# Seven half-width block products in place of eight in the MLP of a decoder block

## The chip, the cores and the metric

One core of one Trainium2 chip runs the whole decoder block in one launch. The metric is the device time of that launch in microseconds (us); less is better. The time before is the median of three runs, and one more execution was profiled.

## What is computed

The block takes x (512 tokens by 1024 channels, float32) and a conditioning vector c. A modulated norm feeds two mixers (a state-space scan and a causal pooling), which gates merge; a projection and a residual follow. Then comes the part that the change touches:

```python
h = rmsnorm(x, norm_mlp_w[i]) * (1.0 + scale_f) + shift_f
x = x + gate_f * (jnp.square(jax.nn.relu(h @ w_up[i])) @ w_down[i])
return rmsnorm(x, norm_final_w)
```

`w_up` is 1024 x 4096 and `w_down` 4096 x 1024, all in float32.

## The kernel before

Channels lie on the 128 partitions and the 512 tokens along the free dimension. TensorE (PE) multiplies float32 data in a format, float32r, that holds fewer bits. So each operand is split into a high part (a cast on ScalarE, ACT) and a low part (the difference, on VectorE, DVE), and each product is made of three: high by high, high by low, low by high (`mm3`, L138 to L142). A column block of 128 outputs over 1024 rows is a `unit` (L144): eight chunks of rows, 24 products of 128 x 128 by 128 x 512, summed in one PSUM bank.

Weights come by `load_unit` (L120): SP issues a load of 512 KB into one of four raw buffers (`RAW`), ACT casts it (L130), DVE subtracts (L131), and the two parts lie in two of the eight buffers of `HL`. A buffer is handed out in the order in which buffers came back, and whoever gets it waits for its last reader. The weights' steps carry a high priority. The order of each engine's queue is laid by the framework's scheduler, from priorities and the order in the program.

PSUM has eight banks. From L617 on all of them are handed out from one list, `PU`.

The MLP (from L706) goes by quarters of the hidden width. In a quarter, eight units of `up` (L713) are made from the modulated activations `h2`; each goes through Relu (ACT, L716), a square (DVE, L708) and a split (L110, L111). Then eight units multiply the quarter's activations `us` with blocks of `w_down`, and `residual` (L659) adds each, times its gate, to `x1` on DVE (L662). The first three `up` units run by halves of the tokens with the rows' chunks outermost (`up_first`, L720), since the second half of the norm is still being worked out; the last three `down` units run by halves too, so that the final norm and the stores of one half lie beside the other half's products (L745 to L760).

The norm ahead (L691 to L701) also goes by halves; `modulate` (L189) makes x * R * scale + shift in two parts, with a temporary tile.

Of the kernel before, what the change touches and what calls it, by code (L numbers as in the profile page):

```python
# [7 lines left out]
F32 = mybir.dt.float32  # L8
# [15 lines left out]
# Columns of the packed per-channel parameters.  # L24
# [11 lines left out]
NSLOT, NRAW, NHL, NPU = 50, 4, 8, 3  # L36
H = T // 2


class Slots:  # L40
    """Buffers of one size, handed out in the order in which they were given back."""
# [17 lines left out]
def block_kernel(tc, xT, crow, arow, par, adaT, wstart, wz, wx, wpool_in, wgate, wpw, wbs, wbp, wout, wup, wdn, out):  # L59
# [3 lines left out]
    with (  # L63
# [6 lines left out]
        def slots(name, n, shape=(P, T), where=sb):  # L70
            def make(i, dt):
                count[0] += 1
                return where.tile(list(shape), dt, tag=f"{name}{i}", name=f"{name}{i}_{count[0]}", bufs=1)
            return Slots(make, n)
# [3 lines left out]
        MT = slots("mt", 3, (P, HG, P))  # L78
        RAW = slots("raw", NRAW, (P, 1024))
        HL = slots("hl", NHL, (P, 1024))  # L80
        SM = slots("sm", 4, (P, NC))
        PU, PS = slots("ps", 8, (P, T), psp), slots("ps", 8, (P, T), psp)
# [8 lines left out]
        cbc = sb.tile([P, DM], F32, name="cbc")  # L91
# [15 lines left out]
        def split(src):  # L107
            """A tile of float32 in two parts that float32r holds exactly."""
            hi, lo = S.get(F32R), S.get(F32R)
            act.copy(hi, src)  # L110
            dve.tensor_tensor(lo, src, hi.bitcast(F32), ALU.subtract)  # L111
            return hi, lo
# [7 lines left out]
        def load_unit(src, n=1024, low=None, at=None, cols=1024):  # L120
            """Blocks of 128 columns of a weight, each in two parts; the buffers are free after their next use."""
            at = at or HL
            with tc.high_priority() if urgent[0] else nullcontext():
                r = RAW.get()
                sp.dma_start(r[:, :n], src)
                blocks, kept = [], []
                for a in range(0, n, cols):
                    w = min(cols, n - a)
                    hi, lo = at.get(F32R), at.get(F32R)
                    act.copy(hi[:, :w], r[:, a:a + w])  # L130
                    (low or dve).tensor_tensor(lo[:, :w], r[:, a:a + w], hi[:, :w].bitcast(F32), ALU.subtract)  # L131
# [56 lines left out]

        def modulate(x, R, scale, shift, hi, lo, t0=0, t1=T):  # L189
            """x * R * scale + shift, in two parts."""  # L190
            t = S.get()
            dve.scalar_tensor_tensor(t[:, t0:t1], x[:, t0:t1], scale, R[:, t0:t1], ALU.mult, ALU.mult)
            act.activation(hi[:, t0:t1], t[:, t0:t1], AF.Identity, bias=shift)
            dve.scalar_tensor_tensor(
                lo[:, t0:t1], t[:, t0:t1], shift, hi[:, t0:t1].bitcast(F32), ALU.add, ALU.subtract)
            S.put(t)

# [8 lines left out]
        def warm(n):  # L206
            """Products of no use that keep the array's clock up."""
# [175 lines left out]
        def bs(g, jp):  # L383
            """Two column blocks of the SSD branch's projection, the rows of one group."""
# [188 lines left out]
        def run(g, fillers):  # L573
            """One group's scan with other units between its steps."""
# [84 lines left out]
        def residual(ps, j, gate, t0=0, t1=T, sums=True, apart=None):  # L659
            """Adds a gated product to x and its squares to the sums."""  # L660
# [12 lines left out]
        def norm(t0, t1, sqs):  # L673
# [3 lines left out]
            bc = rstd(ps, DM, c0, c1, F)  # L677
# [12 lines left out]
        h2 = [(S.get(F32R), S.get(F32R)) for _ in range(8)]  # L690
        for t0, t1 in HALVES:  # L691
# [6 lines left out]
            R = norm(t0, t1, [ssum])  # L698
            for k in range(8):
                modulate(x1[k], R, amod[:, 8 + k:9 + k], mod[:, 24 + k:25 + k], *h2[k], t0, t1)  # L700
# [6 lines left out]
        def squared(u):  # L707
            dve.tensor_tensor(u, u, u, ALU.mult)  # L708
            p = split(u)
            F.put(u)  # L710
            return p

        def up(i):  # L713
            ps = unit(wup[i], h2)
            u = F.get()
            act.activation(u, ps, AF.Relu)  # L716
            PU.put(ps)
            return squared(u)

        def up_first():  # L720
            """The first three units, by halves of the tokens and with the rows' chunks outermost."""
            w = [load_unit(wup[i]) for i in range(3)]
            u = [F.get() for _ in range(3)]
            for t0, t1 in HALVES:
                ps = [PU.get() for _ in range(3)]
                for k in range(8):
                    for i in range(3):
                        mm3(ps[i][:, t0:t1], w[i][k], h2[k], k == 0, k == 7, t0, t1)
                for i in range(3):
                    act.activation(u[i][:, t0:t1], ps[i][:, t0:t1], AF.Relu)  # L730
                PU.put(*ps)
            return [squared(t) for t in u]

        for q in range(4):
            us = up_first() if q == 0 else []
            us += [up(8 * q + i) for i in range(len(us), 8)]
            for j in range(8 if q < 3 else 5):
                ps = unit(wdn[4 * j + q], us)
                residual(ps, j, 40, sums=q == 3)
                PU.put(ps)  # L740
                if q == 3:
                    act.activation(x1[j], x1[j], AF.Copy, scale=col("nfin", j))
            if q < 3:
                free(us)
        w = [load_unit(wdn[4 * j + 3]) for j in (5, 6, 7)]  # L745
        last_sq = F.get()
        for t0, t1 in HALVES:
            for j in (5, 6, 7):
                ps = PU.get()
                for k in range(8):  # L750
                    mm3(ps[:, t0:t1], w[j - 5][k], us[k], k == 0, k == 7, t0, t1)
                residual(ps, j, 40, t0, t1, apart=last_sq if j == 7 else None)
                act.activation(x1[j][:, t0:t1], x1[j][:, t0:t1], AF.Copy, scale=col("nfin", j))
                PU.put(ps)
            R = norm(t0, t1, [ssum, last_sq])
            for j0, j1 in ((0, 2), (2, 4), (4, 6), (6, 8)):
                x = xbig[j0 // 4][:, j0 % 4:j0 % 4 + j1 - j0, t0:t1]
                dve.tensor_tensor(x, x, R[:, t0:t1].unsqueeze(1).broadcast_to([P, j1 - j0, t1 - t0]), ALU.mult)
                sp.dma_start(out[j0:j1, :, t0:t1].rearrange("j p t -> p j t"), x)
            PU.put(R)  # L760
# [71 lines left out]
```

## Time and profile before

| | |
|---|---|
| median of three runs | 1007.04 us (1005.98 to 1007.36) |
| span of the profiled execution (its own time) | 1007.3 us |
| mean granted TensorE clock | 0.996 |
| MLP, from the first full-width `up` unit to the last three units | about 663 to 978 us of the span |
| last three units, final norm and stores | about 978 to 1007 us |
| weights of the MLP | 64 loads of 512 KB, 3.3 us each from issue to landing |

The engines are named PE (TensorE's products), PEld (its weight loads, which overlap the products), DVE, ACT, POOL (GpSimd) and SP (which issues loads). Busy times are shares of the span; rows of slices give tenths of busy time in forty equal pieces. A group of instructions is shown with its line, engine, operation, output and inputs, shapes, count, then its busy time, the mean length of one in ns, and the idle time of the engine ahead of it with what ended that. A timeline row has start, length, engine, line and operation; several equal instructions in a row are merged and counted.

### The profile page before, as it was taken

What the parts mean: (1) busy time and instruction counts of PE and PEld (TensorE: products, weight loads), DVE (VectorE), ACT (ScalarE), POOL (GpSimd) and SP (SyncE); (2) the same over time, 40 slices, a digit from 0 to 9 for tenths busy, and PEclk for the clock granted to TensorE, in tenths of its full rate; (3) what the DMA queues carried; (4) which work ended last, traced back from release to release, by engine and by line L of the source; (5) the groups of instructions that cost most, each with busy time, mean ns of one, the idle gap of its engine ahead of it and who ended that gap; (6) DMA issues with size and microseconds to landing.
All of it is one profiled execution on the core that took longest, in us unless ns stands there. A gap on an engine that the chain in (4) does not pass through costs nothing.

```text
span 1007.3 us, 12196 instructions
## 1 busy us (share of the span) xinstructions
PE 985.8 (98%) x4732; PEld 804.1 (80%) x4732; DVE 623.2 (62%) x887; ACT 482.6 (48%) x718; POOL 85.7 (9%) x79
## 2 busy tenths in 40 slices
PE   9799999999999999999999999999999999999997
PEld 7577777878778878788888888988888888888886
DVE  5978777586777776978765655654344334434444
ACT  5277899579648933453422433442133123213342
POOL 3510310211012012210000000000000000000000
PEclk9999999999999999999999999999999999999998
DMA  9725542452344232437886444032323222232302
GB/s 357 273 89 169 145 126 91 123 130 91 94 129 123 89 111 94 133 102 230 266 266 196 154 161 144 2 126 83 105 86 103 97 92 94 94 105 84 105 1 84
DMA packets 58620, 129.55 MB, mean 129 GB/s; under 512 B 4609, under 2 KB 29313, under 8 KB 58562
## 3 DMA queue, kind: packets, MB, share of 16 engines
q1 hardware_dynamic: 58562, 128.77, 40.0%
q8 instruction: 37, 0.61, 0.2%
q14 instruction: 21, 0.17, 0.1%
HBM read 126.53 MB, written 2.23 MB: 128 GB/s over the span
## 4 chain that ended last, share of the span: by engine, by line
PE 76%; ACT 8%; DVE 7%; DMA 4%; issue 2%; POOL 1%; SPq 1%; DVEq 0%; POOLq 0%; ACTq 0%
PE ps L140 24%; PE ps L141 24%; PE ps L142 24%; DMA mt<-cs_d 3%; ACT hl L130 2%; DVE sz L156 1%; DVE xs L156 1%; ACT L432 1%; PE ps L469 1%; ACT L349 1%; PE ps L453 1%; PE ps L280 1%; DVE hl L131 1%; ACT mt L432 1%; PE ps L446 1%
## 5 line engine op out<-in xcount | busy, mean ns | idle before, releaser
L140 PE MATMUL ps<-s,hl 128*128 128x512 f32 (+1 forms) x1272 | 493.4, 388 | 1.3 <-ACT pad L528 1.2
L141 PE MATMUL ps<-s,hl 128*128 128x512 f32 (+1 forms) x1272 | 488.4, 384 | 0.0
L142 PE MATMUL ps<-s,hl 128*128 128x512 f32 (+1 forms) x1272 | 488.2, 384 | 0.0
L130 ACT CAST hl<-raw 128x1024 fp32r<-128x1024 f32 (+1 forms) x161 | 167.2, 1041 | 285.3 <-PE ps L141 282.6
L140 PEld LDWEIGHTS ps<-s,hl 128*128 128x128 f32 x1272 | 238.9, 188 | 53.3 <-issue 3.5
L142 PEld LDWEIGHTS ps<-s,hl 128*128 128x128 f32 x1272 | 239.0, 188 | 50.2 <-issue 1.0
L141 PEld LDWEIGHTS ps<-s,hl 128*128 128x128 f32 x1272 | 239.1, 188 | 49.4 <-issue 1.4
L131 DVE TENSOR_TENSOR hl<-raw,hl 128x1024 fp32r<-128x1024 f32 x153 | 189.1, 1238 | 130.3 <-ACT hl L130 126.0
L662 DVE SCALAR_TENSOR_TENSOR xs<-ps,mod,xs 128x512 f32<-128x512 f32 (+1 forms) x46 | 31.3, 681 | 110.6 <-PE ps L142 110.5
L110 ACT CAST s<-sz 128x512 fp32r<-128x512 f32 x52 | 31.5, 620 | 52.8 <-DVE sz L708 42.1
L156 DVE CUSTOM_DVE_ANT_0 raw<-raw,cbc,par_t 128x1024 f32<-128x1024 f32 x32 | 40.9, 1279 | 21.2 <-DMA raw<-adaT 21.2
L111 DVE TENSOR_TENSOR s<-sz,s 128x512 fp32r<-128x512 f32 x52 | 35.0, 690 | 22.9 <-ACT s L110 22.9
L432 ACT ACTIVATE mt<-mt,ncs 128x128 f32<-128x128 f32 x128 | 41.7, 392 | 13.6 <-POOL mt L428 13.3
L345 DVE SCALAR_TENSOR_TENSOR s<-ps,par_t,s 128x511 f32<-128x511 f32 (+2 forms) x54 | 40.2, 745 | 7.4 <-ACT s L343 6.8
L280 PE MATMUL ps<-s,hl 128*128 128x512 f32 x144 | 35.1, 397 | 6.4 <-ACT s L265 6.4
L428 POOL TENSOR_SCALAR_AFFINE_SELECT mt<-mt 128x1024 f32<-128x1024 f32 x16 | 19.8, 1244 | 218.0 <-ACT cd L425 117.3
L280 PEld LDWEIGHTS ps<-s,hl 128*128 128x128 f32 x144 | 26.2, 188 | 14.7 <-ACT s L265 9.0
L349 ACT ACT_TABLE_LOAD x19 | 24.4, 1283 | 7.4 <-DVE s L345 7.1
L432 ACT ACT_TABLE_LOAD x20 | 25.7, 1283 | 0.3
L492 POOL TENSOR_TENSOR s<-s 128x256 f32<-128x256 f32 x16 | 17.3, 1082 | 67.9 <-ACT s L491 67.9
L491 ACT ACTIVATE s<-sz 128x512 f32<-128x512 f32 x16 | 10.1, 630 | 26.2 <-DVE sz L490 26.2
L110 ACT CAST s<-s 128x512 fp32r<-128x512 f32 x16 | 9.9, 622 | 25.6 <-DVE s L541 25.3
(164 smaller groups left out, 797.7 us busy)
## 6 DMA issues: line engine op xcount, KB each, us to landing
raw<-adaT SPq DMA_DIRECT2D x32, 512.0 KB, 4.3
raw<-wup SPq DMA_DIRECT2D x32, 512.0 KB, 3.3
raw<-wdn SPq DMA_DIRECT2D x32, 512.0 KB, 3.3
raw<-wx SPq DMA_DIRECT2D x18, 512.0 KB, 3.4
raw<-wz SPq DMA_DIRECT2D x16, 512.0 KB, 4.2
mt<-cs_d SPq DMA_DIRECT2D x16, 512.0 KB, 6.2
raw<-wbs SPq DMA_DIRECT2D x16, 512.0 KB, 3.4
raw<-wgate SPq DMA_DIRECT2D x16, 512.0 KB, 4.0
```

Source lines behind the costliest of these rows:

```text
L110: act.copy(hi, src)
L111: dve.tensor_tensor(lo, src, hi.bitcast(F32), ALU.subtract)
L130: act.copy(hi[:, :w], r[:, a:a + w])
L131: (low or dve).tensor_tensor(lo[:, :w], r[:, a:a + w], hi[:, :w].bitcast(F32), ALU.subtract)
L140: pe.matmul(ps, whi, xhi[:, t0:t1], start=start, stop=False)
L141: pe.matmul(ps, whi, xlo[:, t0:t1], start=False, stop=False)
L142: pe.matmul(ps, wlo, xhi[:, t0:t1], start=False, stop=stop)
L156: dve.tensor_tensor_reduce(r, r, cbc, 1.0, col("b_ada", j), ALU.mult, ALU.add, mod[:, j:j + 1])
L280: pe.matmul(first[u], w[u][i // 2], h[k][i % 2], start=k == 0 and i == 0, stop=k == 7 and i == 2)
L345: dve.scalar_tensor_tensor(t[:, sh:], ps[:, :T - sh], w(3 - sh), t[:, sh:], ALU.mult, ALU.add)
L349: act.activation(o, t, AF.Silu)
L432: act.activation(m[:, i, :], m[:, i, :], AF.Exp, bias=ncs[:, c, g * HG + i:g * HG + i + 1])
```

## The change

Two column blocks are made together. With the rows' chunks taken as even and odd ones and the tokens as two halves, a pair is a product of 2 x 2 blocks by 2 x 2 blocks. In place of eight block products, seven are made, by Winograd's variant of Strassen's scheme, from sums of weight blocks (S1 to S4) and sums of token halves (T1 to T4). A block product is 12 products of 128 x 128 by 128 x 256.

For a pair `prepare` loads a 1 MB weight, laid out by `pairs` on the host, with blocks in the order A21, A11, A12, A22. Two of the weight sums are made by DMAs that add to what lies in the buffer, issued on POOL's queue; two more are sums on DVE. Each of the seven is split in two parts. `sums` makes the token sums on DVE, in place, and splits them; for `h2` that happens once, for the activations in every `up` pair. The square now runs on ACT. The sums of the products are chained in PSUM: a product's result is copied or added, by ACT or DVE, into a bank where the next product goes on adding.

The order of the block products is written in `run_jobs`: `first` of a pair, `close` of the one before, `middle`, `open` of the next, `third`. The first job is `up_first`, now with four blocks by halves. In each quarter the first pair of `down` blocks stays plain (48 products of 512), as do the last four blocks. So 14 pairs of `up` and 10 of `down` change.

The buffers are cut anew: six of the former eight `HL` buffers serve the weights, exactly one pair's six tiles of 1024; A22 has its own two half-size buffers and split tiles. Two PSUM tiles of two banks (`duo`) hold c11 and c12, two banks of one (`AC`) the other two results, and two are left for plain jobs. `hf` keeps the temporaries of `modulate`, from which the float32 activations are made again for the sums.

```diff
+        def sums(u1, u2, t1, t2):
+            dve.tensor_tensor(u1[:, :H], u1[:, :H], u1[:, H:], ALU.subtract)
+            dve.tensor_tensor(u1[:, H:], u2[:, H:], u1[:, H:], ALU.subtract)
+            dve.scalar_tensor_tensor(u2[:, H:], u2[:, H:], -1.0, u1[:, :H], ALU.mult, ALU.subtract)
+            dve.scalar_tensor_tensor(u2[:, :H], u2[:, H:], -1.0, u2[:, :H], ALU.mult, ALU.subtract)
+            two(u1, t1)
+            two(u2, t2)
...
+                y1, y2, y3, y4 = RAW.get(), RAW.get(), RAW.get(), Y4.get()
+                sp.dma_start(y1, w[:, :1024])
+                sp.dma_start(y3[:, T:], w[:, :T])
+                pool.dma_start(y1[:, :T], w[:, 3 * T:], accum_op=ALU.add)
+                pool.dma_start(y3[:, T:], w[:, T:2 * T], accum_op=ALU.add)
+                sp.dma_start(y2[:, T:], w[:, 2 * T:3 * T])
+                sp.dma_start(y4, w[:, 3 * T:])
+                s1, a11 = parts(y1)
+                dve.tensor_tensor(y2[:, :T], y1[:, :T], y1[:, T:], ALU.add)
+                RAW.put(y1)
+                s2, a12 = parts(y2)
+                dve.tensor_tensor(y3[:, :T], y2[:, :T], y2[:, T:], ALU.add)
+                RAW.put(y2)
+                s4, s3 = parts(y3)
+                RAW.put(y3)
+                a22, = parts(y4, T, S)
+                Y4.put(y4)
...
+        def product(ps, a, b, start=False):
+            for m in range(4):
+                w = tuple(x[:, m * P:(m + 1) * P] for x in a)
+                for i, (x, y) in enumerate(((w[0], b[m][0]), (w[0], b[m][1]), (w[1], b[m][0]))):
+                    pe.matmul(ps, x, y, start=start and m == 0 and i == 0, stop=m == 3 and i == 2, skip_group_check=True)
...
+            def open(self):
+                self.be, self.s5 = BE.get(), U5.get()
+                self.c11, self.c12 = self.be[:, 0, :H], self.be[:, 1, :H]
+                product(self.c12, self.a["S1"], self.b["T1"], True)
+                act.copy(self.s5, self.c12)
+            def first(self):
+                self.ac = AC.get()
+                product(self.ac[:, :H], self.a["A11"], self.b["B11"], True)
+                act.copy(self.c11, self.ac[:, :H])
+            def middle(self):
+                product(self.ac[:, :H], self.a["S2"], self.b["T2"])
+                dve.tensor_tensor(self.c12, self.ac[:, :H], self.s5, ALU.add)
+                product(self.c11, self.a["A12"], self.b["B21"])
+            def third(self):
+                product(self.ac[:, :H], self.a["S3"], self.b["T3"])
+                dve.tensor_tensor(self.ac[:, H:], self.ac[:, :H], self.s5, ALU.add)
+                U5.put(self.s5)
+            def close(self):
+                product(self.c12, self.a["S4"], self.b["B22"])
+                self.done(0, self.be[:, :, :H], 1)
+                BE.put(self.be)
+                product(self.ac[:, :H], self.a["A22"], self.b["T4"])
+                self.done(1, self.ac.rearrange("p (a b) -> p a b", a=2), -1)
+                AC.put(self.ac)
...
+        def run_jobs(jobs):
+            last = None
+            jobs[0].prepare()
+            for n, job in enumerate(jobs):
+                after = jobs[n + 1] if n + 1 < len(jobs) else None
+                if after:
+                    after.prepare()
+                if isinstance(job, Pair):
+                    if n == 0 or not isinstance(jobs[n - 1], Pair):
+                        job.open()
+                    job.first()
+                    if last:
+                        last.close()
+                    job.middle()
+                    if isinstance(after, Pair):
+                        after.open()
+                    job.third()
+                    last = job
+                else:
+                    if last:
+                        last.close()
+                    last = None
+                    job.run()
...
+        def activated(q, p, i, ps, sign):
+            u = U.get()
+            act.activation(ab(u), ps, AF.Relu, scale=float(sign))
+            act.activation(u, u, AF.Square)
+            two(u, us[2 * p + i])
+            kept[i] = u
+            if i == 1:
+                sums(kept[0], u, *ust[p])
+                U.put(kept[0], u)
...
+            for k in range(8):
+                act.activation(hf[k], hf[k], AF.Identity, bias=mod[:, 24 + k:25 + k])
+            for m in range(4):
+                sums(*hf[2 * m:2 * m + 2], *h2t[m])
...
+            for b in duo:
+                pe.matmul(b[:, 0, :], h2[0][0][:, :P], h2[0][0], start=True, stop=True)
+            for i in range(4):
+                activated(0, i // 2, i % 2, ab(ps[i]), 1)
...
+        jobs = [Plain(lambda: [load_plain(wup[i // 2], i % 2, *(() if i < 3 else (S, T))) for i in range(4)], up_first)] + [up(0, 2), up(0, 3)]
+        for q in range(3):
+            jobs += [down_plain(q, (0, 1))] + [down(q, p) for p in (1, 2, 3)] + [up(q + 1, p) for p in range(4)]
+        jobs += [down_plain(3, (0, 1)), down(3, 1), down_plain(3, (4,)), Plain(lambda: loads(3, (5, 6, 7)), last_down)]
+        run_jobs(jobs)
```

`two` is an ACT copy into the high part and a DVE difference for the low one. `parts` is `two` on a whole tile of 1024. `done` is `activated` for `up` pairs; for `down` pairs it is one DVE instruction per block that adds the gated result to `x1`, with the negated gate where the sign is -1.

More of the change, by code (lines that the diff above doesn't have):

```diff
@@ L704, in block_kernel @@
             ada(j)
[L707 to L723, printed above, removed]
+        nmod = sb.tile([P, 8], F32, name="nmod")
@@ new lines, in prepare, with parts @@
+        def prepare(w):
+            def parts(y, n=1024, at=HL):
+                hi, lo = at.get(F32R), at.get(F32R)
+                two(y, (hi, lo))
+                at.put(hi, lo)
+                return [(hi[:, o:o + T], lo[:, o:o + T]) for o in range(0, n, T)]
+            with tc.high_priority():
+                y1, y2, y3, y4 = RAW.get(), RAW.get(), RAW.get(), Y4.get()
[15 more added lines that the diff above has]
+                Y4.put(y4)
+            return {"S1": s1, "A11": a11, "S2": s2, "A12": a12, "S4": s4, "S3": s3, "A22": a22}
@@ new lines, in up_first, with up, down, done @@
+            ub.update(moving(us, ust))
+            for b in duo:
+                pe.matmul(b[:, 0, :], h2[0][0][:, :P], h2[0][0], start=True, stop=True)
+            for i in range(4):
+                activated(0, i // 2, i % 2, ab(ps[i]), 1)
+            PU.put(*ps[:2])
+            AC.put(*ps[2:])
+        def up(q, p):
+            return Pair(wup[4 * q + p], hb, lambda i, ps, sign: activated(q, p, i, ps, sign))
+        def down(q, p):
+            def done(i, ps, sign):
+                j = 2 * p + i
+                x = ab(x1[j])
+                g = (mod[:, 40 + j:41 + j], nmod[:, j:j + 1])[sign < 0]
+                dve.scalar_tensor_tensor(x, ps, g, x, ALU.mult, ALU.add)
+                if q == 3:
+                    squares(j)
+            return Pair(wdn[4 * p + q], ub, done)
```

196 lines of the change are left out of this document (145 added, 51 removed).

## The prediction

> **What bounds the kernel now.** I read the page first: its span, its engines, its forty slices and the chain that ended last.
>
> ```profile
> span 1007.3 us, 12196 instructions
> PE 985.8 (98%) x4732; PEld 804.1 (80%) x4732; DVE 623.2 (62%) x887; ACT 482.6 (48%) x718; POOL 85.7 (9%) x79
> ...
> PE   9799999999999999999999999999999999999997
> ...
> DVE  5978777586777776978765655654344334434444
> ACT  5277899579648933453422433442133123213342
> POOL 3510310211012012210000000000000000000000
> ...
> PE 76%; ACT 8%; DVE 7%; DMA 4%; issue 2%; POOL 1%; SPq 1%; DVEq 0%; POOLq 0%; ACTq 0%
> ```
>
> TensorE (PE) has no slice with room in the last third, where the MLP lies; VectorE (DVE) is at 0.3 to 0.4 there, ScalarE (ACT) lower, GpSimd (POOL) empty. So the MLP costs what its products cost. The busy time by stretches gives that price, the timeline that of half-width products:
>
> ```profile
> 663.00:978.00 315.00, 315.00 (x1366) 256.26 (x1365) 132.38 (x150) 98.42 (x125) 0.00 (x0) 1.00 0.28 92
> ```
>
> ```profile
> 978.94 0.28 PE L140 MATMUL ps<-s,hl 128*128 128x256 f32 x1
> 978.94 0.19 PEld L141 LDWEIGHTS ps<-s,hl 128*128 128x128 f32 x1
> 979.05 0.28 PE L141 MATMUL ps<-s,hl 128*128 128x256 f32 x1
> 979.05 0.19 PEld L142 LDWEIGHTS ps<-s,hl 128*128 128x128 f32 x1
> ...
> 987.27 0.29 PE L142 MATMUL ps<-s,hl 128*128 128x256 f32 x1
> ```
>
> ```profile
> 649.79 0.28 PE L140 MATMUL ps<-s,hl 128*128 128x256 f32 x1
> ...
> 656.46 0.28 PE L142 MATMUL ps<-s,hl 128*128 128x256 f32 x1
> ```
>
> The columns of the first are stretch, length, then busy time and count of PE, weight loads, DVE, ACT, POOL, clock, DMA share and GB/s. A 512-wide product takes 315.0 / 1366 = 0.2306 us. The last stage's first half has 72 products 256 wide (three blocks, eight chunks, three products): 8.33 us over 71 steps, 0.117 us. Beside the second norm's work, 57 consecutive ones give 6.67 / 56 = 0.119. I take 0.119: halving the width halves the price, though every product still has its own weight load.
>
> **The products.** A pair of column blocks was 48 products of 512: 11.07 us. It becomes seven block products of 12 products of 256: 84 x 0.119 = 10.0 us (9.8 at 0.117). By the job list 24 of the 32 pairs change: 14 in `up`, 10 in `down`. At PE's pace that is 24 x 1.07 = 25.7 us saved (30 at 0.117). `up_first` runs four blocks by halves, 192 x 0.119 = 22.8 us, where 144 halves and 24 whole ones stood, 17.1 + 5.5 = 22.6: +0.2. The two products that prepare the PSUM banks: +0.5.
>
> **What the other engines must do in those 10 us.** Durations come from the groups of the MLP stretch, the steps of back-to-back ones from the merged timeline.
>
> ```profile
> L131 DVE TENSOR_TENSOR hl<-raw,hl 128x1024 fp32r<-128x1024 f32 x60 | 73.4, 1226 | 78.0 <-ACT hl L130 74.6
> L130 ACT CAST hl<-raw 128x1024 fp32r<-128x1024 f32 x60 | 62.8, 1050 | 177.7 <-PE ps L141 175.5 <-PE ps L142 2.2
> L111 DVE TENSOR_TENSOR s<-sz,s 128x512 fp32r<-128x512 f32 x32 | 22.1, 693 | 19.9 <-ACT s L110 19.9
> L708 DVE TENSOR_TENSOR sz<-sz 128x512 f32<-128x512 f32 x32 | 21.8, 685 | 0.0
> L662 DVE SCALAR_TENSOR_TENSOR xs<-ps,mod,xs 128x512 f32<-128x512 f32 x28 | 21.0, 751 | 87.7 <-PE ps L142 87.7
> L110 ACT CAST s<-sz 128x512 fp32r<-128x512 f32 x32 | 19.9, 621 | 42.1 <-DVE sz L708 42.1
> L716 ACT ACTIVATE sz<-ps 128x512 f32<-128x512 f32 x29 | 17.1, 591 | 0.0
> ...
> L669 ACT ACTIVATE sz<-xs 128x512 f32<-128x512 f32 x3 | 1.9, 634 | 0.0
> ...
> L192 DVE SCALAR_TENSOR_TENSOR s<-xs,amod,ps 128x256 f32<-128x256 f32 x3 | 1.3, 475 | 0.0
> L730 ACT ACTIVATE sz<-ps 128x256 f32<-128x256 f32 x3 | 0.9, 379 | 0.0
> ```
>
> ```profile
> 647.60 1.27 DVE L194 SCALAR_TENSOR_TENSOR s<-s,mod,s 128x256 fp32r<-128x256 f32 x3
> ...
> 658.10 3.50 DVE L131 TENSOR_TENSOR hl<-raw,hl 128x1024 fp32r<-128x1024 f32 x3 [4.80 <-ACT hl L130]
> 661.52 1.89 DVE L708 TENSOR_TENSOR sz<-sz 128x512 f32<-128x512 f32 x3
> ```
>
> Three in a row of 1226 ns end after 3.50 us, so the step is (3.50 - 1.23) / 2 = 1.14; likewise 0.60 for 512 elements and 0.39 for 256. A full DVE queue is priced by steps, one that waits before every instruction by durations.
>
> DVE, an `up` pair: three differences of 1024 and one of 512 for the weights (4.02), two weight sums of 512 (1.20), two 256-wide PSUM adds (0.78), two differences of the activation (1.20), four 256-wide sums (1.56), two more differences (1.20): 9.96 us by steps, 11.4 by durations. A `down` pair has two residuals of 0.75 in place of the last three terms: 7.5 us. ACT, an `up` pair, by durations: casts 3 x 1.05 + 0.62, PSUM copies 2 x 0.38, Relu 2 x 0.59, Square 2 x 0.63, four casts of 0.62: 9.45. So the room that the slices show is used up: DVE equals PE in `up` and is at three quarters in `down`; ACT keeps a little.
>
> When DVE falls behind, its inputs are there and the steps apply, so I choose near the steps: an `up` pair at 10.4 us (bounds 9.9 and 11.4), a `down` pair at 10.05. 24 x 11.07 = 265.7 becomes 14 x 10.4 + 10 x 10.05 = 246.1: -19.6 us.
>
> **New waits on PE.** Inside a row of pairs each read of a bank lies under other products: after `first` come the 24 of `close`; after S2 the 24 of A12 and the next `open`; after S3 the next `first` and S4: each 2.86 us for an add of 0.48 or a copy of 0.38, with perhaps one 1.14 us difference ahead on the queue. Where a pair follows a plain job, nothing lies between `first` and S2: PE waits for the copy, 0.38 and some 0.2 of hand-over, 0.6 x 5 places = 3.0. Where a plain job follows a pair, S3's add has S4 alone over it, 1.43 us: beside a busy DVE I put 0.2 x 5 = 1.0 (0 to 3).
>
> With six weight buffers, exactly one pair, y1 of the next pair is cast only once A11 is done; `close` and `middle` (5.7 us) cover 1.05 + 1.23. After `up_first`, whose chunks are outermost, its first block frees its buffers nine products (1.1 us) before the end, so the first pair waits about 1.3. The token sums for h2t follow the second norm's work on DVE:
>
> ```profile
> 646.42 1.26 DVE L192 SCALAR_TENSOR_TENSOR s<-xs,amod,ps 128x256 f32<-128x256 f32 x3 [0.90 <-PE ps L184]
> ...
> 652.41 0.89 DVE L194 SCALAR_TENSOR_TENSOR s<-s,mod,s 128x256 fp32r<-128x256 f32 x2 [0.19 <-ACT s L193]
> ```
>
> From 653 on 16 sums and 8 differences take 16 x 0.39 + 8 x 0.60 = 11.0 us, to 664; `up_first` covers that, as its 22.8 us from 646 on end at 669. But its four blocks are activated all at once under the first pair: 7.9 us of sums and differences, 5.2 of weights and 0.8 of adds, 13.9 us of DVE against 10.0 of PE. The next pair, with a plain job's weights to prepare, recovers the 3.9. I count 1.5 (0 to 4).
>
> Behind a waiting add on DVE's queue stand the next weights, behind the copy on ACT's the casts of y3 and the Relus: a late add delays the weights that PE wants 5.7 us later, and those have room. The last stage keeps its halves and its norm; its third block takes the buffers of block 4, and two half blocks, 5.7 us, cover that split: nothing.
>
> **The loads.** Per pair 1.75 MB in place of 1.0, some 180 GB/s where the stretch above had 92. Two of the transfers add into a buffer and go through POOL, whose queue is otherwise empty here; no row shows such a transfer. The nearest:
>
> ```profile
> raw<-wup SPq DMA_DIRECT2D x32, 512.0 KB, 3.3
> ...
> sz<-adaT SPq DMA_DIRECT2D x8, 512.0 KB, 9.5
> ...
> s<-xT SPq DMA_DIRECT2D x8, 256.0 KB, 4.3
> ...
> out<-xs SPq DMA_DIRECT2D x8, 256.0 KB, 2.3
> ```
>
> The bounds are 2.3 and 9.5 us; I take 4.3, a 256 KB load beside others. With four raw buffers y1 of a pair takes y3's of two pairs earlier. That loop (load 3.3, add, split 2.3, S1 to the following S4 5.7, split 2.3) is 13.6 us plus the add, and has 20.0: it stalls nothing up to 6.4 us, so zero here. On SP's queue y3's load waits for the y2 buffer of the pair before; load and add (7.6 us) then end about 5 us ahead of their use. On POOL's queue each add waits for its load, and nothing stands behind but the next add.
> No row has the price of a software-issued transfer; the Trainium skill ("DMA: Bandwidth & Descriptors", Anatomy of one DMA) gives about 2.0 us plus the bytes at 436 GB/s. That is an estimate of 2.6 us, and the sum stays as it is.
>
> **The sum.** Against the profiled execution's span, 1007.3, the only time it has (the median is 1007.04): -19.6 + 0.2 + 0.5 + 3.0 + 1.0 + 1.3 + 1.5 = -12.1, so 995.2, and on the median's scale 994.9. Forecast 995, its own range 985 to 1002.
>
> **Rivals.**
> *Nothing waits* (0.13): DVE keeps its steps in all pairs, products run at 0.117 and the edges hide. 24 x (11.07 - 9.83) = 29.8 saved, a few us of edges: 981. For it: PE's rate in the quiet stretch. Against: DVE's 9.96 against 9.83.
> *DVE becomes the bound in `up`* (0.13): each step waits for its cast, 11.4 us a pair: 14 us more than forecast, 1009, no change to speak of. For it: 74.6 us of L131's idle time was waiting for ACT. Against: that DVE had nothing else to do.
> *The adding transfer is late* (0.10), the case on the slow side: over 6.4 us each us costs half a us per pair. From 7.4 us on (12 us over 24 pairs are 0.5 each) the gain is gone; at 9.5 us it is 1.55 x 24 = 37 us on 995: 1032. For it: two transfers in series and a buffer loop over two pairs. Against: the DMA share in the MLP row is 0.28.
> *The order is not the written one* (0.03): the scheduler lays the queues; if the covering products aren't in between, three hand-overs of about 0.6 per pair are bare: 43 us, 1038.
> *Weight loads don't hide* (under 0.01): the rows above start a load of 0.19 us every 0.11 us beside matmuls at the same step. If each load stood alone, a pair would cost 84 x (0.119 + 0.188) = 25.8 against 48 x (0.231 + 0.188) = 20.1 us: 137 us slower than now, 1144.
> The Trainium skill ("TensorE: Matmul & The Clock Gate", Part 3) says that a weight load overlaps running matmuls only where the row groups differ; these loads have all 128 rows. By it the last rival would hold; the trace disagrees, with 0.117 us a product.
>
> **Chances.** The forecast has 0.60. Faster by over 0.2% (about what a measurement of this kernel can tell from no change) means under 1005: forecast, the first rival and a third of the second, 0.77. Within 0.2%: 0.05, out of the second. Slower: 0.18, the rest of the second and the last three. The range, 981 to 1011, leaves out the last three (0.14) and the fast edge of the first (0.06).
>
> **What would show it.** Right: in the stretch of `up` pairs DVE busy nine tenths and more, PE with gaps of under 1 us before products that follow a PSUM add, and about 10.4 us a pair; in `down` about 10.05 and DVE near three quarters; a gap of about 0.6 us on PE at each change from plain job to pair; about 4 us from the adding transfer's issue to its landing. Wrong: PE waiting for weight differences all through `down` (transfer late); a matmul step over 0.125 us; or `up` pairs at 11 us and more.

## The result, and the profile after

| | before | after |
|---|---|---|
| median of four runs each | 1006.92 us (1005.98 to 1007.36) | 1104.74 us (1101.89 to 1107.79) |
| span of the profiled execution | 1007.3 us | 1106.1 us |
| mean granted TensorE clock | 0.996 | 0.961 |

The ratio is 1.098 (95% interval 1.096 to 1.100): the change costs a tenth. The forecast was 995, the range 981 to 1011, and none of the rivals gave this time. The page of the changed kernel, with the lines that answer to those of before:

```profile
span 1106.1 us, 14849 instructions
...
PE 1002.7 (91%) x5622; PEld 856.7 (77%) x5622; DVE 741.3 (67%) x1121; ACT 577.6 (52%) x892; POOL 125.5 (11%) x127
...
PE   8899999999999999998999987898879888887896
...
DVE  6985976667677688877456559565575567555763
ACT  5277987697498234541133337543464346434652
POOL 3600221110120122000000000001101110011000
PEclk9999999999999999999999989899999998988998
```

PE, at nine tenths and more in every slice of the last third but the very last before, stands mostly at seven to nine tenths there now. DVE is at five to seven tenths up to the last slice: no engine is full there. A stage in which nothing is full is bound by waits, so the next thing to look for is who waits for whom.

First, in which stage the time lies. The second norm ends and the final norm begins with products on a tile of ones; these rows of the timeline (start, length, engine, line, operation) give both edges, first before, then after:

```profile
645.68 0.70 PE L184 MATMUL ps<-sz,ones 128*128 128x256 f32 x2
...
987.40 0.28 PE L166 MATMUL ps<-zeros,ones 128*128 128x2 f32 x2
```

```profile
664.21 0.64 PE L195 MATMUL ps<-sz,ones 128*128 128x256 f32 x2
...
1082.12 0.28 PE L177 MATMUL ps<-zeros,ones 128*128 128x2 f32 x2
```

The second of each pair of norm products starts at 646.0 and 664.5. So 18.5 us are lost ahead of the MLP, which the prediction had not priced at all; the MLP goes from 341.4 to 417.6 us, 76.2 more; the rest goes from 19.9 to 24.0. Together that is 98.8. The MLP by stretches (stretch, length, then busy time and count of PE, weight loads, DVE, ACT, POOL, clock, DMA share, GB/s), before and after:

```profile
646.00:987.40 341.40, 341.40 (x1562) 281.46 (x1561) 147.12 (x177) 110.71 (x149) 0.00 (x0) 1.00 0.26 87
```

```profile
664.50:1082.10 417.60, 349.30 (x2447) 327.56 (x2446) 265.39 (x406) 204.49 (x321) 39.05 (x46) 0.93 0.45 115
```

PE idled for none of the 341.4 us before and for 68.3 of the 417.6 after, and the clock fell from 1.00 to 0.93. The waits of that stage (engine and line, what it waited for, us in total, times, longest):

```profile
ACT d L733 <- DMA d<-wup: 57.5, 12, 7.9
...
DVE d L773 <- DMA d<-wdn: 34.1, 10, 5.6
...
PE ps L792 <- ACT duo L810: 22.6, 9, 4.7
PE ps L792 <- DVE ps L819: 21.8, 10, 5.6
```

ACT stands before a cast of weights and DVE before a weight sum because a transfer isn't there, and PE stands before a PSUM copy (L810) and a PSUM add (L819) of these same engines. One lap in a row of pairs shows how the two hang together; the rows are those of the timeline, in order of time:

```profile
885.33 1.22 DVE L734 TENSOR_TENSOR d<-d,d 128x1024 fp32r<-128x1024 f32 x1
...
886.58 0.33 SPq L766 DMA_DIRECT2D d<-wup  x1
...
891.48 0.85 POOL L768 DMA_DIRECT2D d<-wup  x1 [7.10 <-DMA d<-wup]
...
893.88 1.58 PE L792 MATMUL ps<-s,s 128*128 128x256 f32 x12
...
896.44 1.04 ACT L733 CAST d<-d 128x1024 fp32r<-128x1024 f32 x1 [5.58 <-DMA d<-wup]
...
897.39 0.37 ACT L810 COPY duo<-ps 128x256 f32<-128x256 f32 x1
...
897.69 1.03 ACT L733 CAST d<-d 128x1024 fp32r<-128x1024 f32 x1
897.70 2.35 DVE L734 TENSOR_TENSOR d<-d,d 128x1024 fp32r<-128x1024 f32 x2
...
897.81 2.93 PE L792 MATMUL ps<-s,d 128*128 128x256 f32 x12 [2.35 <-ACT duo L810]
...
898.95 0.33 SPq L770 DMA_DIRECT2D d<-wup  x1
...
900.08 0.33 SPq L766 DMA_DIRECT2D d<-wup  x1
...
910.33 1.04 ACT L733 CAST d<-d 128x1024 fp32r<-128x1024 f32 x1 [4.09 <-DMA d<-wup]
```

The split of a y3 ends on DVE at 886.55, and 0.03 us later SP issues the load of a y1 (L766), that of the pair after the next, which takes y3's buffer. 4.9 us on, at 891.48, it is there and POOL issues the adding transfer (L768). That lands 4.9 us later; ACT, idle for 5.58 us ahead of it, casts this y1 at 896.44. Behind that cast, on ACT's queue, have stood c11's copy (897.39), for which PE waits, and the cast of the y3 that comes one pair after the first (897.69). Its split ends at 900.05, and at 900.08 the following y1's load starts. The lap, 13.5 us, is 4.9 + 4.9 + 3.7: a ring of a buffer and an in-order queue, once per pair, where PE's work is 10. SP's queue would close it nearly as soon: a load of a y2 (L770), which takes the buffer of the y1 just split, stands there ahead of the next y1's load, and it is issued at 898.95, 12.4 us after 886.58.

The gap costs more than itself. The stretch in front of the wait, the one behind it, and the next:

```profile
889.00:897.80 8.80, 6.46 (x55) 6.25 (x53) 2.97 (x5) 2.41 (x4) 1.42 (x2) 1.00 0.47 120
897.80:901.20 3.40, 3.39 (x16) 3.39 (x17) 3.28 (x4) 3.40 (x7) 0.29 (x1) 0.50 0.59 110
901.20:905.00 3.80, 3.80 (x34) 3.80 (x34) 3.55 (x7) 3.05 (x6) 0.00 (x0) 1.00 0.70 246
```

For 3.4 us after a gap of 2.35 us the granted clock is 0.50, and 16 products are done in place of some 29. PE's busy time of the last experiment below, whose clock reads 1.00, is 324.0 us in this stage; here it is 349.3. With that kernel as the measure of the products alone, the sum of the MLP is: 341.4 - 17.4 (fewer products) + 25.3 (slow clock) + 68.3 (idle) = 417.6.

The transfers themselves, in the MLP (count, KB each, median us to landing):

```profile
d<-wup POOLq DMA_DIRECT2D x26, 256.0 KB, 4.3
d<-wup SPq DMA_DIRECT2D x12, 512.0 KB, 4.4
d<-wdn POOLq DMA_DIRECT2D x20, 256.0 KB, 5.1
```

### The profile page after: what moved, and what is told of

Same layout as the page of the kernel before. It is cut to its first block, busy times and chain, and to the rows that moved or that the text cites. A ratio compares the mean times of both kernels' runs of the same rounds, so it can differ in the third digit from the quotient of the medians.

```text
span 1106.1 us, 14849 instructions
## 1 busy us (share of the span) xinstructions
PE 1002.7 (91%) x5622; PEld 856.7 (77%) x5622; DVE 741.3 (67%) x1121; ACT 577.6 (52%) x892; POOL 125.5 (11%) x127
## 5 line engine op out<-in xcount | busy, mean ns | idle before, releaser
L151 PE MATMUL ps<-s,d 128*128 128x512 f32 (+1 forms) x670 | 261.0, 390 | 2.9 <-ACT pad L530 1.7
L152 PE MATMUL ps<-s,d 128*128 128x512 f32 (+1 forms) x670 | 256.8, 384 | 0.0
L153 PE MATMUL ps<-s,d 128*128 128x512 f32 (+1 forms) x670 | 256.0, 383 | 0.0
L733 ACT CAST d<-d 128x1024 fp32r<-128x1024 f32 x87 | 90.4, 1047 | 154.9 <-DMA d<-wup 61.7
L141 ACT CAST d<-d 128x1024 fp32r<-128x1024 f32 (+1 forms) x97 | 100.1, 1034 | 106.0 <-PE ps L152 55.0
L151 PEld LDWEIGHTS ps<-s,d 128*128 128x128 f32 x670 | 125.8, 188 | 31.2 <-issue 3.3
L142 DVE TENSOR_TENSOR d<-d,d 128x1024 fp32r<-128x1024 f32 x89 | 111.4, 1254 | 57.2 <-ACT d L141 56.7
L152 PEld LDWEIGHTS ps<-s,d 128*128 128x128 f32 x670 | 126.0, 188 | 25.5 <-issue 2.2
L153 PEld LDWEIGHTS ps<-s,d 128*128 128x128 f32 x670 | 125.9, 188 | 25.6 <-issue 0.9
L734 DVE TENSOR_TENSOR d<-d,d 128x1024 fp32r<-128x1024 f32 x87 | 105.2, 1221 | 49.8 <-ACT d L733 49.5
L792 PE MATMUL ps<-s,d 128*128 128x256 f32 x654 | 98.2, 301 | 27.6 <-ACT duo L810 22.6
L792 PEld LDWEIGHTS ps<-s,d 128*128 128x128 f32 x654 | 90.1, 207 | 30.4 <-ACT duo L810 24.4
L792 PE MATMUL duo<-s,d 128*128 128x256 f32 x684 | 99.0, 291 | 13.6 <-ACT d L733 4.0
L792 PEld LDWEIGHTS duo<-s,d 128*128 128x128 f32 x684 | 90.4, 197 | 18.3 <-ACT d L733 4.9
L773 DVE TENSOR_TENSOR d<-d 128x512 f32<-128x512 f32 x24 | 16.6, 692 | 79.9 <-DMA d<-wdn 34.1
L151 PE MATMUL duo<-s,d 128*128 128x512 f32 (+1 forms) x135 | 53.8, 402 | 4.1 <-DVE xs L627 4.0
L152 PE MATMUL duo<-s,d 128*128 128x512 f32 (+1 forms) x135 | 53.3, 395 | 0.0
L153 PE MATMUL duo<-s,d 128*128 128x512 f32 (+1 forms) x135 | 52.8, 392 | 0.0
L434 ACT ACTIVATE d<-d,ncs 128x128 f32<-128x128 f32 x128 | 41.9, 392 | 10.6 <-POOL d L430 10.4
```

Of the source, the lines that this page charges most:

```text
L151: pe.matmul(ps, whi, xhi[:, t0:t1], start=start, stop=False)
L152: pe.matmul(ps, whi, xlo[:, t0:t1], start=False, stop=False)
L153: pe.matmul(ps, wlo, xhi[:, t0:t1], start=False, stop=stop)
L434: act.activation(m[:, i, :], m[:, i, :], AF.Exp, bias=ncs[:, c, g * HG + i:g * HG + i + 1])
L733: act.copy(dst[0], src)
L734: dve.tensor_tensor(dst[1], src, dst[0].bitcast(F32), ALU.subtract)
```

## The experiments

Theory T is the ring above. Its rivals: R1, the adding transfers as such are too many or too slow; R2, DVE or ACT are simply full. T4 and R4 concern the 18.5 us ahead of the MLP. In the expectations, "85 us of gaps and 27 us of slow clock" are a rougher count than the 68.3 and 25.3 above, from the starts of neighbouring products between 640 and 1085 us of the changed kernel: a long step's excess over the product's own price is a gap, a short one's is slow clock. Each experiment is one run with its profile; the kernel before took 1005.96 to 1008.08 us beside them. The four runs of the changed kernel span 5.9 us, so a difference of that size between two single runs says little. The changed kernel's profile is of its slowest run, 1107.79 us; its row has the median and that profile. The results together, MLP meaning from the second norm's last product on ones to the final norm's first:

| kernel | us | second norm ends | MLP | PE busy in it | clock in it |
|---|---|---|---|---|---|
| before | 1005.96 to 1008.08 | 646.0 | 341.4 | 341.4 | 1.00 |
| changed | 1104.74 | 664.5 | 417.6 | 349.3 | 0.93 |
| no add into y1 | 1039.71 | 659.9 | 355.5 | 332.1 | 0.97 |
| no add into y3 | 1084.65 | 666.0 | 394.5 | 340.0 | 0.95 |
| y1's cast behind y3's | 1097.07 | 664.2 | 408.6 | 346.3 | 0.93 |
| both queues | 1070.81 | 663.4 | 382.0 | 338.6 | 0.96 |
| sums on GpSimd | 1094.02 | 662.1 | 406.6 | 345.3 | 0.94 |
| slots reordered | 1047.27 | 661.1 | 360.9 | 330.1 | 0.98 |
| banks apart | 1085.24 | 650.8 | 412.6 | 348.0 | 0.91 |
| queues and banks | 1044.94 | 655.1 | 367.8 | 331.3 | 0.97 |
| the same, sums on GpSimd | 1041.21 | 648.9 | 371.2 | 336.1 | 0.95 |
| slots, banks, first pair | 1026.72 | 652.1 | 352.5 | 326.3 | 0.99 |
| the same, sums on GpSimd | 1025.08 | 648.7 | 355.3 | 330.8 | 0.97 |
| and y2's sum behind the add | 1022.34 | 653.3 | 347.5 | 326.7 | 0.98 |
| the same, sums on GpSimd | 1017.32 | 649.7 | 346.0 | 324.0 | 1.00 |

**One add away.**

```diff
-                pool.dma_start(y1[:, :T], w[:, 3 * T:], accum_op=ALU.add)
```

> Left out: the adding transfer into y1 (the last column group's half of S1's weight sum). Theory T (a ring): y1's load, its adding transfer, y1's cast, y3's cast queued behind it on ScalarE, y3's split and the next y1's load, which takes y3's slot, close in one lap of about 13.9 us per pair. Without the add the lap is 13.9 - 4.9 = 9.0 us, under PE's 10.3, so 24 pairs fall from about 14.1 to 10.3: 91 us less, about 1015 us (1005 to 1030), and ScalarE's and GpSimd's waits for DMA go. Rival R1 (the two adding transfers as such: traffic and GpSimd's queue): half of the two goes, so about half of the 90 us: 1060, and the same for the other add. Rival R2 (VectorE or ScalarE are simply full): no change, about 1105.

```diff
-                pool.dma_start(y3[:, T:], w[:, T:2 * T], accum_op=ALU.add)
```

> Left out: the adding transfer into y3 (the second column group's half of the weight sum behind S3 and S4). Theory T: it lies beside the ring of y1, not in it, so little moves: 1085 to 1105 us, and ScalarE still waits for y1's add. Rival R1 (the adding transfers as such): as without the add into y1, about 1060. Rival R2 (VectorE or ScalarE full): no change, about 1105.

Without y1's add 65 us go, without y3's 20. The two transfers are alike in size and queue, so R1, which wanted 45 and 45, falls; R2 falls too. T had the order right and the size wrong: the first time is 10 us above its range (1005 to 1030), the second just under its own (1085 to 1105). It had put all of the stage's loss on the ring, and 355.5 us are still 14 above the MLP before.

**The queue's order alone.** The next pair's y1 is held behind this pair's y3, on ACT:

```diff
+                with tc.issue_after(y3_cast.pop()) if y3_cast else nullcontext():
-                s1, a11 = parts(y1)
+                    s1, a11 = parts(y1)
...
                 s4, s3 = parts(y3)
+                y3_cast.append(casts[-1])
```

> Everything is computed; only the order on ScalarE's queue changes: the next pair's y1 cast stands behind this pair's y3 cast (and so behind c11's copy). Theory T: the ring then closes over two pairs, as the prediction had reckoned, and y3's slot comes free without waiting for the next y1: PE's pace, 24 x (14.1 - 10.3) = 91 us less, about 1015 us (1005 to 1040), the same transfers notwithstanding. Rival R1 (the transfers as such are too many or too slow): no change, 1095 to 1110. Rival R2 (VectorE or ScalarE full): no change.

A miss: 8 us, little more than the spread of the changed kernel's runs. The waits of this kernel's MLP say why:

```profile
PE ps L798 <- DVE ps L825: 43.1, 19, 5.6
DVE d L778 <- DMA d<-wup: 32.7, 12, 3.8
DVE d L778 <- DMA d<-wdn: 29.0, 10, 5.7
```

ACT no longer heads the list; the same wait has moved to DVE, where the next pair's y2 sum (L778, it needs y1 with its add) stands ahead of y3's split and of the PSUM add L825. The theory was mended: the ring closes through either queue. So both are opened, by the same means:

```diff
+                cast, rest = y3_cast.pop() if y3_cast else (None, None)
+                with tc.issue_after(cast) if cast else nullcontext(), tc.issue_after(rest) if cast else nullcontext():
-                s1, a11 = parts(y1)
-                dve.tensor_tensor(y2[:, :T], y1[:, :T], y1[:, T:], ALU.add)
+                    s1, a11 = parts(y1)
+                    dve.tensor_tensor(y2[:, :T], y1[:, :T], y1[:, T:], ALU.add)
```

> Everything is computed; the next pair's y1 cast stands behind this pair's y3 cast on ScalarE, and the next pair's y2 sum behind this pair's y3 split on VectorE. Theory T, mended after the order on ScalarE alone gave 8 us: the ring closes through either in-order queue (a y2 sum that waits for y1's add stands ahead of y3's split on VectorE too), so both have to be opened. Then the loop runs over two pairs, and PE's 85 us of gaps and 27 us of slow clock in the MLP shrink to about 30 and 12 as they did without the add into y1: 1025 us (1010 to 1050). Rival R1 (the adding transfers as such are too slow or too many): no change from the order on ScalarE alone, 1090 to 1105.

34 us go, with the same transfers and the same instructions: against R1. It is also less than T gave, 21 us above its range. The lap is 12 us in place of 13.5 (y1's loads at 856.78, 868.73 and 880.62), and in it PE waits for a difference (0.35 us before 869.89) and a residual (1.1 before 872.45) on DVE. That holding y1 behind y3 is what keeps the lap at 12 was not tried by itself.

**No adding transfer.**

```diff
-                sp.dma_start(y3[:, T:], w[:, :T])
-                pool.dma_start(y1[:, :T], w[:, 3 * T:], accum_op=ALU.add)
-                pool.dma_start(y3[:, T:], w[:, T:2 * T], accum_op=ALU.add)
-                sp.dma_start(y2[:, T:], w[:, 2 * T:3 * T])
                 sp.dma_start(y4, w[:, 3 * T:])
+                sp.dma_start(y2[:, T:], w[:, 2 * T:3 * T])
+                pool.tensor_tensor(y3[:, T:], y1[:, :T], y1[:, T:], ALU.add)
+                pool.tensor_tensor(y1[:, :T], y1[:, :T], y4, ALU.add)
```

> Everything is computed; the two weight sums are made by GpSimd's tensor additions of 512 from buffers that are loaded anyway, with no adding transfer and 1.0 MB per pair in place of 1.75; the queues' order is left to the scheduler as in the changed kernel. Theory T: the lap loses the add's 4.9 us and gains two additions of about 1.4 us each: 13.9 - 4.9 + 2.8 = 11.8 us against PE's 10.3: about 1045 us (1030 to 1065). Rival R1 (the transfers as such): as without both, under 1035. If GpSimd's additions hold VectorE up at a shared port, VectorE's own additions grow longer and it is over 1065.

A miss for both, and the clearest word against R1: with no adding transfer and 73 GB/s in the MLP in place of 115, 11 us go. The third branch, a shared port, had the right side (over 1065), but DVE's busy time in the MLP grows by 9.6 us only, its 1024-wide differences keep their mean (1221 ns, 1220 before), and the same sums cost nothing in the kernels further down. The waits of this kernel, 690 to 1060 us:

```profile
POOL d L769 <- DVE d L734: 211.3, 18, 20.5
...
ACT d L733 <- POOL d L770: 40.3, 18, 3.8
```

L769 makes y3's sum and needs the buffer that the pair before's y2 gives back late; L770, y1's sum, stands behind it on POOL's queue, and ACT waits for L770. By these rows the ring has a third queue to close through.

**The slots alone.** The same instructions, the same transfers, no order forced; only the buffers are given back in another sequence, so that the next y1 no longer takes y3's:

```diff
-                RAW.put(y1)
                 s2, a12 = parts(y2)
                 dve.tensor_tensor(y3[:, :T], y2[:, :T], y2[:, T:], ALU.add)
-                RAW.put(y2)
                 s4, s3 = parts(y3)
-                RAW.put(y3)
+                RAW.put(y3, y1, y2)
```

> Everything is computed, with the same instructions; only the order in which a pair gives its three raw buffers back changes, to y3, y1, y2, so that the next pair's y2 takes y3's slot, its y3 takes y1's and the y1 after that takes y2's. Theory T (the ring y3's slot, y1's load, y1's add, y1's cast, y3's cast behind it): y1's load no longer waits for a y3 split, the ring is cut, and the MLP's 85 us of gaps and 27 us of slow clock fall to 40 and 15 or less: about 1045 us (1020 to 1070). Rival R1 (the adding transfers as such): no change, 1090 to 1110. Rival R2 (VectorE or ScalarE full): no change.

1047.27 where 1045 was expected: 57 us of the MLP's 76. This settles that the loop through the buffers cost the time: neither the number of transfers nor any engine's work changed, and the adding ones landed no sooner on the whole (medians 5.3 and 4.5 us here, 4.3 and 5.1 before). On ACT the wait shrinks from 57.5 us to this (690 to 1020 us):

```profile
ACT d L733 <- DMA d<-wup: 21.4, 10, 3.5
```

**The banks.** The changed kernel puts banks 4 to 7 into two tiles of two banks for its whole length. A place ahead of the MLP, where PE stops in a unit:

```profile
518.94 0.39 PE L151 MATMUL duo<-s,d 128*128 128x512 f32 x1
...
522.59 0.68 DVE L627 TENSOR_TENSOR xs<-xs,duo 128x512 f32<-128x512 f32 x1
...
523.32 0.80 PE L151 MATMUL duo<-s,d 128*128 128x512 f32 x1 [3.99 <-DVE xs L627]
```

```diff
-        duo = [psp.tile([P, 2, T], F32, name=f"duo{i}") for i in range(2)]
...
+        duo = [[bank(4 + 2 * i + j, F32) for j in range(2)] for i in range(2)]
...
-                self.c11, self.c12 = self.be[:, 0, :H], self.be[:, 1, :H]
+                self.c11, self.c12 = self.be[0][:, :H], self.be[1][:, :H]
...
-                self.done(0, self.be[:, :, :H], 1)
+                self.done(0, (self.c11, self.c12), 1)
```

> Everything is computed; PSUM banks 4 to 7 are four tiles in place of two two-bank ones over the whole kernel (a pair's first block is then evacuated in two instructions of 256). Theory T4: the 18 us lost ahead of the MLP come from units in the two banks of one tile waiting for each other's evacuation: the lag at the second norm falls from 18 to under 5 us, about 1088 us in all. Rival R4 (the MLP's loads and splits, put at high priority, get in the way earlier): no change ahead of the MLP, about 1105.

As T4 had it. The rows of this kernel:

```profile
650.51 0.64 PE L191 MATMUL ps<-sz,ones 128*128 128x256 f32 x2
...
1063.36 0.28 PE L173 MATMUL ps<-zeros,ones 128*128 128x2 f32 x2
```

13.7 of the 18.5 us ahead of the MLP go and 3.9 of the 4.1 behind it (1083.5 - 1063.4 = 20.1). That the two banks of one tile cost this is shown; that a unit waits for the evacuation of the unit in its tile's other bank is read from the row at 523.32 and not tried by itself. What the last 4.8 us ahead of the MLP are stays open.

**Together.** Both queues and the banks, then the same with sums on GpSimd (the edits above, combined):

> Everything is computed; both queues' order as in the kernel with both queues mended, and banks 4 to 7 as four tiles. Theories T and T4 together: the two gains add up, 1025 - 19 = about 1005 us (990 to 1030). If the transfers as such bound the MLP: about 1075.

> Everything is computed; both queues' order, banks 4 to 7 as four tiles, and the two weight sums on GpSimd in place of the adding transfers. Theory T: with the ring open the sums' way matters little, within 15 us of the same kernel with adding transfers: about 1000 us (985 to 1020). Rival R1 (the adding transfers as such): over 40 us faster than that kernel.

The two gains do add (34 and 20 make 54, 60 were measured), but the queues' own run had stayed 46 us above its expectation, and these stay 40 above theirs with it, outside both ranges. The way of the sums matters little, 4 us, as T has it.

Next the slots in place of the queues, and in `up_first` the two banks evacuated first that the first pair needs. In the changed kernel the first pair waits like this:

```profile
683.10 1.21 PE L792 MATMUL duo<-s,d 128*128 128x256 f32 x8 [1.00 <-DVE d L734]
687.56 0.80 PE L792 MATMUL duo<-s,d 128*128 128x256 f32 x2 [3.25 <-DVE s L734]
692.31 2.93 PE L792 MATMUL ps<-s,d 128*128 128x256 f32 x12 [3.95 <-ACT pad L887]
696.16 0.80 PE L792 MATMUL duo<-s,d 128*128 128x256 f32 x2 [0.92 <-ACT d L733]
```

```diff
-            ps = [PU.get(), PU.get(), AC.get(), AC.get()]
+            ps = [AC.get(), AC.get(), PU.get(), PU.get()]
```

> Everything is computed: the raw buffers given back in the order y3, y1, y2, banks 4 to 7 as four tiles, and up_first evacuating the two banks first that the first pair needs. T and T4 add up: 1045 - 20, and about 8 us for the first pair's wait of over 5 us with the slow clock behind it: 1015 us (990 to 1040). If only the transfers' time counts: 1075.

> Everything is computed: as the kernel with slots, banks and first pair mended, with the two weight sums on GpSimd in place of the adding transfers. T: the ring is cut either way, so within 15 us of it, on the lower side since y1 is whole 6 us after its slot comes free in place of 10: 1005 us (985 to 1030). Rival R1: over 40 us faster than that kernel.

Both lie within their ranges, 12 and 20 us above what was expected, and 2 us apart from each other, which is against R1 once more. Last, y2's sum and what follows from it behind the PSUM add:

```diff
-                dve.tensor_tensor(self.c12, self.ac[:, :H], self.s5, ALU.add)
+                self.add = dve.tensor_tensor(self.c12, self.ac[:, :H], self.s5, ALU.add).ins
...
                     job.middle()
+                    if isinstance(after, Pair):
+                        after.split(job.add)
```

> Everything is computed: the kernel with slots, banks and first pair mended, and on VectorE the next pair's y2 sum and what follows from it stand behind this pair's PSUM add into C12. Theory T (queued waits): PE's waits for PSUM adds, 5 us, and for weight differences, 9 us, shrink with the slow clock behind them: 1012 us (1002 to 1020). Rival R2 (VectorE full in `up`): no change, 1022 to 1030.

> Everything is computed: the same order on VectorE in the kernel with the weight sums on GpSimd. Theory T: the five waits of about 2 us for a PSUM add go, with the slow clock behind them, 9 + 8 us: 1008 us (998 to 1018). Rival R2 (VectorE full in `up`): no change, 1020 to 1030.

4 us with adding transfers, which lies in R2's "no change" (1022 to 1030); 8 us without them, at the upper edge of T's range and under R2's. So this pair doesn't settle whether the last waits are queued ones or DVE being full in `up`; that stays open. The last kernel is the best, 1017.3, and still 1.1% slower than the one before (1006.21 beside it). It loses 3.7 us ahead of the MLP and 4.6 in it. Its PE needs 324.0 us for the MLP and idles for 22; the kernel before needs 341.4 and idles for none. A cost of its own is that GpSimd's additions lengthen DVE's differences (whether PE's last waits come from that wasn't tried). DVE's groups from 690 to 990 us, in this kernel and in the one with adding transfers:

```profile
L730 DVE TENSOR_TENSOR d<-d,d 128x1024 fp32r<-128x1024 f32 x77 | 104.8, 1367 | 12.5 <-ACT d L729 11.9
```

```profile
L730 DVE TENSOR_TENSOR d<-d,d 128x1024 fp32r<-128x1024 f32 x76 | 92.3, 1222 | 27.1 <-ACT d L729 26.9
```

## Why the prediction was wrong

**The step that failed** is in its part on loads: "That loop (...) is 13.6 us plus the add, and has 20.0: it stalls nothing up to 6.4 us, so zero here." It let y3's split wait for buffers and products alone and so gave the loop two pairs. On ACT's queue the cast of y3 stands behind the next pair's y1 cast, which waits for its own load and add, and that load had waited for the y3 before. The loop therefore closes within one pair: 4.9 + 4.9 + 3.7 = 13.5 us of 10, where the text had 20. Cutting it by the buffers' order alone gave back 57 of the MLP's 76 us. The prediction did say, just before, what stands behind a waiting add and a waiting copy; it did not ask what stands behind a cast that waits for a transfer. The rival of the late adding transfer named the ring's parts, but hung on a duration over 6.4 us; the adds landed in 4.3 and 5.1 (medians), close to the 4.3 chosen, and of 48 only two took over 6.4 (6.8). The rival on the scheduler's order looked at PE's queue; it was the order on ACT's, DVE's and POOL's that counted.

**Not in the sum at all.** Losing the clock: a term for a wait was its length, and behind most gaps of over 2 us came 3.4 us and more at half clock, which cost 25 us in the MLP. The stages ahead of the MLP: the diff showed that banks 4 to 7 became two tiles for the whole kernel, and the text priced only the two products that prepare them, at 0.5 us; the tiles cost 13.7 ahead and 3.9 behind.

**Mis-sized.** After `up_first` the prediction counted 1.3 and 1.5 us. PE waited 1.00 + 3.25 + 3.95 + 0.92 = 9.1 us in the rows above. The 3.95 come because the first pair's second block needs a bank whose evacuation stands third in line. The 3.25 are for one of the last differences of the token sums; the prediction had these done by 664 under `up_first`, and this row stands behind the first pair's weights on DVE, after `up_first` has ended at 681:

```profile
686.82 1.29 DVE L734 TENSOR_TENSOR s<-sz,s 128x512 fp32r<-128x512 f32 x2
```

At the changes from pairs to plain jobs it had 0.2 us each (0 to 3 in all). There, too, a sum that waits for the next pair's transfer stands ahead on DVE (L773), and S3's add (L819) and PE stand behind it:

```profile
822.98 0.69 DVE L773 TENSOR_TENSOR d<-d 128x512 f32<-128x512 f32 x1 [5.59 <-DMA d<-wdn]
...
827.08 2.93 PE L792 MATMUL ps<-s,s 128*128 128x256 f32 x12 [5.56 <-DVE ps L819]
```

**Right.** Halving the width halves the price: in the lap 12 products of 256 take (1.58 - 0.28) / 11 = 0.118 us each at full clock, 0.119 was taken, with a weight load each. The rule of the Trainium skill ("TensorE: Matmul & The Clock Gate", Part 3) by which such loads would not overlap does not hold in this trace either. PE's work in the MLP did fall, by 17 us at least. And DVE was not the bound: in the MLP it was busy for 265 of 417.6 us, and the slots alone gave 57 us with DVE's work unchanged. Of its own signs of being wrong, "`up` pairs at 11 us and more" was seen: c11's copies of two `up` pairs stand at 897.39 and 911.29, 13.9 us apart. PE did wait in `down` too, but mostly for a PSUM copy and a PSUM add, not for weight differences.

The estimate from the Trainium skill ("DMA: Bandwidth & Descriptors", Anatomy of one DMA), 2.6 us for the adding transfer, was low: 4.3 and 5.1 were measured, beside other traffic. The measurement decides.

## What to carry to other kernels

Where a buffer is refilled for the next round, walk the loop through every in-order queue, not through data alone: whatever stands at the head of a queue and waits for a transfer holds back all that stands behind it, and if what stands behind frees the buffer that the transfer's successor needs, the loop closes a round early. Before forcing an order or blaming the transfer, look at which use's buffer the late load takes: handing buffers back in another sequence gave seven times what forcing the order on one queue gave. And price a gap on PE with the slow clock behind it.

## What the hardware showed besides

Gaps and clock: take the PE waits in the profiles of the changed kernel and all thirteen experiments, from 690 to 990 us, that began at full clock. Of 112 waits of 0.9 to 1.6 us none was followed by a lower clock (a fall up to 2 us behind its end), of 34 of 1.6 to 2.5 us 21 were, and of 47 of 2.5 us and more 45 were, for 3.4 us or a multiple of it at 0.50. The Trainium skill ("TensorE: Matmul & The Clock Gate", Part 1) names an idle window of about 3.4 us for the fall to half clock and as long for the return. The return agrees (897.8 to 901.2 above); the fall came here after 2.35 us.

GpSimd beside DVE: a 1024-wide difference that overlaps an addition of GpSimd can take up to twice as long. In the last kernel, from 650 us on, the 38 that overlap one by over 0.3 us took 1.21 to 2.31 us, the 67 that overlap none at most 1.23. One of the longest:

```profile
776.04 1.67 POOL L771 TENSOR_TENSOR d<-d 128x512 f32<-128x512 f32 x1 [15.88 <-DVE d L730]
776.49 2.31 DVE L730 TENSOR_TENSOR d<-d,d 128x1024 fp32r<-128x1024 f32 x1
```

2.31 against a mean of 1.22 where GpSimd only issues transfers. The Trainium skill ("SBUF — State Buffer", Who interferes with whom) says that a VectorE instruction with two SBUF inputs contends with a GpSimd instruction that reads SBUF; the trace agrees.
